# The issue order of all engines in a hybrid four-branch encoder block, computed with the framework's timeline model in place of its default model

## Chip, cores and metric

The kernel runs on one core of one Trainium2 chip. The metric is the time of one execution on the device, in microseconds. Five engines take part: TensorE (PE; its weight loads are shown as PEld), VectorE (DVE), ScalarE (ACT), GpSimd (POOL) and SyncE (SP), which here only issues DMAs. Each engine works off its own list of instructions strictly from the front; an instruction that needs a result of another engine waits for a semaphore, and everything behind it on that engine waits too.

## What is computed

One layer of a streaming encoder on 512 tokens of width 1024, float32 throughout. Cut to what matters:

```
h = rms_norm(x, norm_mix)
proj = h @ w_in                        # feeds four token mixers and four gates
y_ssd, y_lru, y_ret, y_rwkv = mamba2(...), rglru(...), retention(...), rwkv7(...)
merged = sum over m of sigmoid(gate_m) * (y_m @ w_branch[m])
x = x + merged @ w_out
h = rms_norm(x, norm_ffn)
x = x + (silu(conv(h @ up_gate)) * conv(h @ up_val)) @ w_down
return rms_norm(x, norm_final)
```

The part that matters here is rwkv7: per head, a state is carried from token to token. The kernel does this in 8 chunks of 64 tokens, one chunk after the other.

## The kernel before

**Products.** Every weight block is loaded by a DMA on SP's queue into `raw` (L106, four buffers), cast to fp32r by ACT into `whi` (L100) and its rest computed by DVE into `wlo` (L101); there are three buffers of each. A product is three matmuls (L119, L120, L121) for each of the 8 slices of the inner dimension, 128x128 weights against 512 columns, so 24 matmuls to a block, summed in a PSUM tile `acc` (three buffers). In the tail of the program (output projection, feed-forward) the same is done by lines 240 to 242 and 949 to 951. All other matmuls are plain fp32 and small; the profile counts two instructions for each of them.

**Rounds.** `rwkv` runs over 8 pairs of heads (j = 0 to 7, called rounds here). A round is:

- `rwkv_a1`: three projections (r, k, v), a norm (L313, then the square root on eight columns, L132 to L136), two small products (L125, L126).
- `rwkv_a2`: 16 fp32 matmuls (L372) whose results go through DRAM (writes L415, reads L418) into `nt`; then **the substitution**, 31 pairs of DVE instructions (L424, L426), each needing the one ahead of it, and a copy (L428); its result goes through DRAM again (L432, L433, L438, L441) into `x11` and `tt`.
- `rwkv_b`: 16 small matmuls (L452), a copy, 16 more (L462), a copy, and then **the chain** of 8 chunks. In a chunk PE does L480 (twice), DVE copies (L482), PE does L484, ACT and then DVE copy (L485, L486), PE does L488, DVE adds (L491), and that is the input of the next chunk's L480. Behind the chain stand 8 matmuls (L497), a norm on DVE (L506 to L514), a transpose (L96, into `rb`), a gate product and a write to DRAM (L246).

```
for c in range(NCH):
    nc.tensor.matmul(ps[...], g[:, c, e], sv[:, c, e, :], ...)      # L480
    nc.vector.tensor_copy(out=pp[:, c], in_=ps[...])                # L482
    nc.tensor.matmul(sk[:, 0:P], tt[:, c, :], pp[:, c], ...)        # L484
    nc.scalar.copy(out=sv[0:64, c, 0], in_=sk[0:64, 0:64])          # L485
    nc.vector.tensor_copy(out=sv[64:128, c, 1], in_=sk[64:128, ..]) # L486
    nc.tensor.matmul(sk[:, P:2 * P], bt[:, c, :], sv[:, c], ...)    # L488
    nc.vector.tensor_tensor(out=sv[h, c + 1, e], ..., op=ALU.add)   # L491
```

**Filler.** Between the rounds `fill(us)` pulls pieces of other work from a generator: the other three mixers, and then gates and branch products of those three (`branch`, which reads a mixer's output back from DRAM, L872, splits it into `yh` and `yl`, and multiplies it). Only the fourth branch product (`branch(3, 3, merged)`) needs the rounds' output; its inner slice 7 needs round 7. After it come the output projection, a norm, and the feed-forward products.

**What sets the order.** The code is traced into a program, and the framework then orders it. It plays the program on a model of the machine: whenever an engine of the model is free, it takes of the instructions whose inputs are there the one traced first, and the order in which that happens is the order in which each engine's instructions are issued on the chip. The times that `fill` is given and the order of the mixers only set the order of tracing. The model is chosen where the program's context is opened:

## Time and profile before

| | |
|---|---|
| median of 3 runs | 1616.52 us (1614.81 to 1617.13) |
| the profiled execution | 1615.14 us, of which the span from first to last instruction is 1613.4 us |
| PE busy in the span | 1562.6 us |
| DVE, ACT, POOL busy | 1047.2, 719.7, 141.2 us |
[...]

Busy means that at least one instruction of the engine was under way. Consecutive matmuls overlap, so the start of the next one tells what a matmul costs, and the duration doesn't. Waits are put down to what ended last.

### The profile page before, as it was taken

What the parts mean: (1) busy time and instruction counts of PE and PEld (TensorE: products, weight loads), DVE (VectorE), ACT (ScalarE), POOL (GpSimd) and SP (SyncE); (2) the same over time, 40 slices, a digit from 0 to 9 for tenths busy, and PEclk for the clock granted to TensorE, in tenths of its full rate; (3) what the DMA queues carried; (4) which work ended last, traced back from release to release, by engine and by line L of the source; (5) the groups of instructions that cost most, each with busy time, mean ns of one, the idle gap of its engine ahead of it and who ended that gap; (6) DMA issues with size and microseconds to landing.
All of it is one profiled execution on the core that took longest, in us unless ns stands there. A gap on an engine that the chain in (4) does not pass through costs nothing.

```text
span 1613.4 us, 22510 instructions
## 1 busy us (share of the span) xinstructions
PE 1562.6 (97%) x8452; PEld 1279.7 (79%) x8452; DVE 1047.2 (65%) x2302; ACT 719.7 (45%) x1188; POOL 141.2 (9%) x190
## 2 busy tenths in 40 slices
PE   7899999899999999999999999999999999999998
PEld 7787778787788788877788778788888888888886
DVE  6787697875886788878636757544435665656233
ACT  6453466445753576258422432323223544444122
POOL 1200202202101201201200300100000000000000
PEclk9999999999999999999999999999999999999999
DMA  5233133232243234433533323444222223233231
GB/s 205 92 122 99 56 118 91 76 107 87 87 125 97 77 105 116 125 105 101 163 105 105 118 91 99 133 140 142 91 92 92 94 92 104 91 102 106 95 102 53
DMA packets 108461, 169.47 MB, mean 105 GB/s; under 512 B 54832, under 2 KB 64304, under 8 KB 108352
## 3 DMA queue, kind: packets, MB, share of 16 engines
q1 hardware_dynamic: 107632, 166.92, 33.0%
q8 instruction: 66, 1.08, 0.3%
q10 hardware_dynamic: 720, 1.11, 0.2%
q14 instruction: 43, 0.35, 0.1%
HBM read 150.66 MB, written 15.24 MB: 103 GB/s over the span
## 4 chain that ended last, share of the span: by engine, by line
PE 79%; DVE 14%; ACT 3%; issue 2%; POOL 1%; DMA 1%; SPq 0%; DVEq 0%; ACTq 0%; POOLq 0%
PE acc L119 17%; PE acc L120 17%; PE acc L121 17%; PE acc L949 3%; PE acc L951 3%; PE acc L950 3%; DVE wlo L101 2%; PE rb L480 2%; PE acc L242 2%; PE acc L241 2%; PE acc L240 2%; PE ra L372 1%; PE rb L488 1%; PE inn L96 1%; PE ra L96 1%
## 5 line engine op out<-in xcount | busy, mean ns | idle before, releaser
L119 PE MATMUL acc<-hh,whi 128*128 128x512 f32 (+1 forms) x1240 | 487.3, 393 | 0.0
L120 PE MATMUL acc<-hh,wlo 128*128 128x512 f32 (+1 forms) x1240 | 486.0, 392 | 1.2 <-DVE wlo L101 1.1
L121 PE MATMUL acc<-hl,whi 128*128 128x512 f32 (+1 forms) x1240 | 485.9, 392 | 0.0
L101 DVE TENSOR_TENSOR wlo<-raw,whi 128x1024 fp32r<-128x1024 f32 x228 | 279.1, 1225 | 169.7 <-ACT whi L100 168.8
L100 ACT CAST whi<-raw 128x1024 fp32r<-128x1024 f32 x228 | 237.8, 1045 | 205.9 <-PE acc L951 86.5
L120 PEld LDWEIGHTS acc<-hh,wlo 128*128 128x128 f32 x1240 | 234.3, 189 | 45.6 <-issue 2.2
L119 PEld LDWEIGHTS acc<-hh,whi 128*128 128x128 f32 x1240 | 234.3, 189 | 44.6 <-issue 2.2
L121 PEld LDWEIGHTS acc<-hl,whi 128*128 128x128 f32 x1240 | 234.2, 189 | 44.3 <-issue 1.8
L1004 DVE SCALAR_TENSOR_TENSOR fc<-acc,fw,fc 128x511 f32<-128x511 f32 x88 | 65.9, 749 | 76.5 <-ACT fc L1002 75.0
L119 PE MATMUL acc<-yh,whi 128*128 128x512 f32 x256 | 102.4, 400 | 0.0
L120 PE MATMUL acc<-yh,wlo 128*128 128x512 f32 x256 | 101.1, 395 | 0.0
L121 PE MATMUL acc<-yl,whi 128*128 128x512 f32 x256 | 100.9, 395 | 0.0
L477 POOL TENSOR_SCALAR sd<-sv,dl 64x64 f32<-64x64 f32 x112 | 57.4, 513 | 351.4 <-DVE sv L491 338.0
L1002 ACT ACTIVATE fc<-acc,fw 128x512 f32<-128x512 f32 x44 | 34.3, 779 | 93.9 <-PE acc L121 93.9
L240 PE MATMUL acc<-whi,hh 128*128 128x256 f32 (+1 forms) x256 | 74.8, 293 | 0.4 <-ACT whi L100 0.4
L241 PE MATMUL acc<-wlo,hh 128*128 128x256 f32 (+1 forms) x256 | 74.4, 291 | 0.0
L242 PE MATMUL acc<-whi,hl 128*128 128x256 f32 (+1 forms) x256 | 74.1, 290 | 0.0
L949 PE MATMUL acc<-whi,gh 128*128 128x512 f32 x176 | 69.4, 395 | 0.0
L951 PE MATMUL acc<-whi,gl 128*128 128x512 f32 x176 | 69.4, 395 | 0.0
L950 PE MATMUL acc<-wlo,gh 128*128 128x512 f32 x176 | 69.4, 395 | 0.0
L878 ACT ACTIVATE gt<-acc 128x512 f32<-128x512 f32 x32 | 19.0, 597 | 91.0 <-PE acc L121 91.0
L424 DVE TENSOR_TENSOR prod<-nt,xr 128x60 f32<-128x60 f32 (+24 forms) x248 | 54.0, 218 | 5.5
(329 smaller groups left out, 2404.8 us busy)
## 6 DMA issues: line engine op xcount, KB each, us to landing
raw<-in_wts_dram SPq DMA_DIRECT2D x226, 512.0 KB, 3.3
yr<-y SPq DMA_DIRECT2D x32, 256.0 KB, 2.8
y<-sm SPq DMA_DIRECT2D x24, 256.0 KB, 2.2
nt<-nd SPq DMA_DIRECT2D x32, 128.0 KB, 3.2
sm<-acd SPq DMA_DIRECT2D x16, 256.0 KB, 3.6
x<-in_x_dram SPq DMA_DIRECT2D x4, 512.0 KB, 5.3
ym<-bg SPq DMA_DIRECT2D x16, 128.0 KB, 1.8
sm<-sm SPq DMA_DIRECT2D x32, 64.0 KB, 2.0
```

The source lines that it names most:

```text
L100: nc.scalar.copy(out=hi, in_=src)
L101: nc.vector.tensor_tensor(out=lo, in0=src, in1=hi.bitcast(F32), op=ALU.subtract)
L119: nc.tensor.matmul(ps, wh, xh, start=first, stop=False)
L120: nc.tensor.matmul(ps, wl, xh, start=False, stop=False)
L121: nc.tensor.matmul(ps, wh, xl, start=False, stop=last)
L240: nc.tensor.matmul(o, hh[:, ko, t], wh[:, s], start=ko == 0, stop=False)
L241: nc.tensor.matmul(o, hh[:, ko, t], wl[:, s], start=False, stop=False)
L242: nc.tensor.matmul(o, hl[:, ko, t], wh[:, s], start=False, stop=ko == KT - 1)
L949: nc.tensor.matmul(ps[i], xh[:, ko, t], w[0][:, s], start=ko == 0, stop=False)
L950: nc.tensor.matmul(ps[i], xh[:, ko, t], w[1][:, s], start=False, stop=False)
L951: nc.tensor.matmul(ps[i], xl[:, ko, t], w[0][:, s], start=False, stop=ko == 2 * nblk - 1)
L1004: nc.vector.scalar_tensor_tensor(out=t[:, s:], in0=ps[:, :S - s], scalar=fw[:, o + 2 - s:o + 3 - s], in1=t[:, s:], op0=ALU.mult, op1=ALU.add)
```

## The change

The context is opened with another model, the framework's timeline simulation, which follows sequencers, queues and engines more finely than the default one:

```diff
-    with _tile.TileContext(nc) as tc:
+    with _tile.TileContext(nc, schedule_with_timeline_sim=True) as tc:
         tile_hybrid_block(tc, *args)
```

The matmuls, vector operations, activations and DMAs are the same ones; ACT loads its function tables 65 times in place of 64, and instructions that only wait for a semaphore follow from the new order. The order differs on every engine, from the first norm to the last product. Three places are shown.

**Round 7, first chunk, on PE.** `g`, `sv`, `tt`, `bt`, `nt` belong to the chain, `acc` to the products. Before:

```order
L462 MATMUL rb<-tt,x_9774 32x32
L480 MATMUL rb<-sv,g 128x64 x2
L121 MATMUL acc<-hl,whi 128x512
L462 MATMUL rb<-tt,x_9774 32x32 x15
L119 MATMUL acc<-hh,whi 128x512
L120 MATMUL acc<-hh,wlo 128x512
L121 MATMUL acc<-hl,whi 128x512
L119 MATMUL acc<-hh,whi 128x512
L484 MATMUL rb<-nt,tt 128x128
```

And now:

```order
L121 MATMUL acc<-yl,whi 128x512 x2
L452 MATMUL rb<-x_9774,ab 32x32 x16
L462 MATMUL rb<-tt,x_9774 32x32 x16
L480 MATMUL rb<-sv,g 128x64 x2
L484 MATMUL rb<-nt,tt 128x128
L488 MATMUL rb<-sv,bt 128x128
L480 MATMUL rb<-sv,g 128x64 x2
```

The products that stood between the steps of this chain stand ahead of it; all 8 chunks of round 7 follow each other as the first one does.

**End of round 7, on PE.** `o` is the normed output of the round, `glh` the gate, `yh` the operand of the branch products. After the change:

```order
L480 MATMUL rb<-sv,g 128x64 x2
L484 MATMUL rb<-nt,tt 128x128
L497 MATMUL rb<-sv,gb 128x128 x8
L96 MATMUL rb<-ident,o 128x128 x4
L119 MATMUL rb<-glh,lh_10173 128x512
L120 MATMUL rb<-glh,ll_10174 128x512
L121 MATMUL rb<-gll,lh_10173 128x512
L119 MATMUL acc<-yh,whi 128x512
```

The `yh` of the last row is slice 7 of the fourth branch product, which is round 7's own output read back from DRAM; before the change gates and branch products of other mixers stood at each of these places.

**Substitution of round 5, on DVE.** `prod`, `nt`, `xr` belong to the substitution, `kss`, `knr`, `knu` to the norm of round 6's `rwkv_a1`. Before:

```order
L424 TENSOR_TENSOR prod<-nt,xr 128x18x4
L426 TENSOR_TENSOR xr<-xr,prod 128x18x4
L424 TENSOR_TENSOR prod<-nt,xr 128x17x4
L426 TENSOR_TENSOR xr<-xr,prod 128x17x4
L424 TENSOR_TENSOR prod<-nt,xr 128x16x4
L426 TENSOR_TENSOR xr<-xr,prod 128x16x4
```

And now:

```order
L101 TENSOR_TENSOR wlo<-raw,whi 128x1024
L315 TENSOR_SCALAR kss<-ra 128x8
L424 TENSOR_TENSOR prod<-nt,xr 128x17x4
L132 TENSOR_SCALAR knr<-kss 128x8
L426 TENSOR_TENSOR xr<-xr,prod 128x17x4
L134 SCALAR_TENSOR_TENSOR knu<-knr,kss 128x8
L424 TENSOR_TENSOR prod<-nt,xr 128x16x4
L135 TENSOR_TENSOR knu<-knu,knr 128x8
L426 TENSOR_TENSOR xr<-xr,prod 128x16x4
```

The norm of the next round and weight splits have moved in between the pairs of the substitution.

## Rows read from the trace of the kernel before

**Rows 1.** The page: busy time of each engine, and the chain that ended last.
```profile
PE 1562.6 (97%) x8452; PEld 1279.7 (79%) x8452; DVE 1047.2 (65%) x2302; ACT 719.7 (45%) x1188; POOL 141.2 (9%) x190
...
PE 79%; DVE 14%; ACT 3%; issue 2%; POOL 1%; DMA 1%; SPq 0%; DVEq 0%; ACTq 0%; POOLq 0%
```

**Rows 2.** Waits of PE: engine, line, waited for: total us, times, longest us.
```profile
PE inn L96 <- DVE nxn L157: 10.2, 1, 10.2
PE ra L372 <- DVE bk L357: 4.5, 1, 4.5
...
PE rb L488 <- DVE sv L486: 3.8, 4, 2.3
...
PE rb L497 <- DVE sv L486: 1.5, 1, 1.5
...
PE rb L480 <- DVE sv L491: 1.2, 3, 0.7
...
PE rb L484 <- DVE nt L482: 1.0, 3, 0.4
```

**Rows 3.** Timeline of PE, round 7: start us, duration us, engine, line, tiles, [wait].
```profile
962.55 1.05 PE L372 MATMUL ra<-g,bk 128*128 128x128 f32 x8
963.36 0.48 PE L121 MATMUL acc<-hl,whi 128*128 128x512 f32 x1
963.68 0.40 PE L119 MATMUL acc<-hh,whi 128*128 128x512 f32 x1
963.91 0.39 PE L120 MATMUL acc<-hh,wlo 128*128 128x512 f32 x1
...
1008.31 0.28 PE L452 MATMUL rb<-x,ab 32*32 32x32 f32 x2 [0.18 <-DMA x<-xd]
```

**Rows 4.** Timeline of DVE, round 7's substitution, first instruction and last.
```profile
977.27 0.21 DVE L424 TENSOR_TENSOR prod<-nt,xr 128x31 f32<-128x31 f32 x1
...
998.61 0.41 DVE L428 COPY prod<-xr 128x256 f32<-128x256 f32 x1
```

**Rows 5.** Groups of DVE from 970 to 999 us: count, busy us, mean ns, idle ahead.
```profile
L424 DVE TENSOR_TENSOR prod<-nt,xr 128x60 f32<-128x60 f32 (+24 forms) x31 | 6.7, 215 | 0.9
...
L101 DVE TENSOR_TENSOR wlo<-raw,whi 128x1024 fp32r<-128x1024 f32 x5 | 6.1, 1222 | 2.9 <-ACT whi L100 2.6 <-issue 0.3
```

**Rows 6.** Timeline of SP's queue, round 7: the four reads into nt.
```profile
966.41 1.71 SPq L418 DMA_DIRECT2D nt<-nd  x4
```

**Rows 7.** DMA issues: count, KB each, median us from issue to landing.
```profile
yr<-y SPq DMA_DIRECT2D x32, 256.0 KB, 2.8
...
nt<-nd SPq DMA_DIRECT2D x32, 128.0 KB, 3.2
...
y<-yu SPq DMA_DIRECT2D x8, 256.0 KB, 2.4
```

**Rows 8.** Timeline of PE, round 5: a chunk without products between its steps.
```profile
774.79 0.49 PE L484 MATMUL rb<-nt,tt 128*128 128x128 f32 x2
777.58 0.49 PE L488 MATMUL rb<-sv,bt 128*128 128x128 f32 x2 [2.30 <-DVE sv L486]
778.38 0.84 PE L480 MATMUL rb<-sv,g 128*128 128x64 f32 x4 [0.31 <-DVE sv L491]
779.60 0.80 PE L484 MATMUL rb<-nt,tt 128*128 128x128 f32 x2 [0.38 <-DVE nt L482]
```

**Rows 9.** Timeline of PE, round 5: the shortest step from L484 to L488.
```profile
785.69 0.38 PE L484 MATMUL rb<-nt,tt 128*128 128x128 f32 x2
...
786.69 0.49 PE L488 MATMUL rb<-sv,bt 128*128 128x128 f32 x2
```

**Rows 10.** Stretch 779 to 785.6 us: PE, PEld, DVE, ACT, POOL busy, clock, DMA.
```profile
779.00:785.60 6.60, 6.22 (x20) 5.16 (x20) 2.81 (x8) 0.74 (x3) 1.32 (x3) 0.50 0.41 138
```

**Rows 11.** Timeline of PE, end of round 7.
```profile
1045.69 1.09 PE L497 MATMUL rb<-sv,gb 128*128 128x128 f32 x8
...
1054.94 0.63 PE L96 MATMUL rb<-ident,o 128*128 128x128 f32 x4 [0.40 <-DVE o L514]
```

**Rows 12.** Timeline of SP's queue, end of round 7: the write of its output.
```profile
1057.93 0.33 SPq L246 DMA_DIRECT2D y<-yu  x1
```

## Prediction, written before the changed kernel ran

> **What bounds the kernel now.** I read the page first: PE is busy for 1562.6 of 1613.4 us and the chain that ended last runs through PE for 79% [rows 1], so the time is PE's work plus PE's waits. The list of PE's waits is short: its 23 groups add up to 44.3 us. Of these 10.2 are the first transpose waiting for the first norm, which no order avoids; the steps of the chain of chunks cost 3.8, 1.5, 1.2 and 1.0, together 7.5; the other 26.4 are waits ahead of L372, of transposes and of small matmuls, the largest 4.5 [rows 2]. L452, which needs the whole substitution and four DMA trips, waited once, for 0.18 us [rows 3]. So the old order hides the rounds almost wholly, and a new order can win little but lose much. I then read from the changed order how much PE work stands between the ends of each dependence, and from the trace how long the dependence takes. PE work is priced by starts: a product matmul of 512 columns is 0.23 us (963.68 to 963.91), four fp32 matmuls of 128 columns 0.81 to 0.89 (962.55 to 963.36, or to their end less the overlap) [rows 3].
>
> **Part 1: from L372 to L452.** This stretch is: the last L372 ends at 963.60 [rows 3]; four reads into nt are issued from 966.41 on, the last 1.3 later, and land 3.2 after their issue [rows 6, 7]: 7.3 us. Then the substitution. From its first instruction at 977.27 to the end of the copy at 999.02 [rows 4] it takes 21.75; its own instructions are 31 pairs of 0.215 each and the copy, 13.7 [rows 4, 5], and the others that stand between the first and the last of them in DVE's order, each at its own duration in the trace (a weight split 1.22 [rows 5]), are 6.9. So it takes what DVE has in that piece of its list, plus 1. From there to L452 at 1008.31 are another 9.3 [rows 3, 4]. The bill is therefore 17.6 + own + others. In the order before it is never more than the PE work that stands between L372 and L452: rounds 0 to 7 have 69, 50, 46, 59, 57, 53, 51 and 45 us of it against bills of 67, 48, 40, 55, 43, 46, 36 and 38, which agrees with the one wait of 0.18.
>
> In the changed order PE has 48.7, 63.5, 51.1, 43.1, 58.4, 39.6, 54.9 and 23.6 us there. Own work is unchanged, but others are now 26.6, 36.7, 29.4, 22.3, 29.6, 17.5, 21.0 and 4.8 us: the norm of the next round's a1, its scan and its splits stand between the pairs. The bills become 59.7, 67.9, 60.7, 53.4, 60.9, 48.7, 52.4 and 36.1. Bill less work: 11.0, 4.4, 9.6, 10.3, 2.5, 9.1, 0 and 12.5, together 59 us of new waits at L452. Bounds: 45, if each of the seven trips through DRAM that count here is 2 us shorter than in round 7; 80, if L424 also waits for what stands ahead of it, as in round 7 of before, where it began some 6 us after its data (966.41 + 1.3 + 3.2 = 970.9 against 977.27) [rows 4, 6, 7].
>
> **Part 2: chunks without cover.** Between the steps of the chain the old order has at least one product matmul, but for three steps. In the new one 24 steps to L480, 19 to L488 and 20 to L484 follow directly, 22 of these 63 in round 7, 41 in rounds 0 to 5. What such a step costs is seen at 774.79: 2.79 us to L488, less 0.22 of work; 0.80 to L480, less 0.22; 1.22 to L484, less 0.34 [rows 8]. That is the upper end, 2.57, 0.58 and 0.88. The shortest step to L488 in the trace took 1.00, less 0.22 [rows 9], and for the others I take the mere waits, 0.31 and 0.38 [rows 8], as lower end. Sums: 24 x 0.31 + 19 x 0.78 + 20 x 0.38 = 30, and 13.9 + 48.8 + 17.6 = 80. In round 7 no other instruction stands between the chain's own on DVE, so I go nearer to the lower end: 0.5, 1.2 and 0.6, together 47. Less the 7.5 that the chain waits now [rows 2]: 39 (22 to 73).
>
> The rest of the chains is the reverse: in round 6 a whole product block, some 5 us, stands between any two steps. That costs nothing by itself but delays the round: its chain takes 118 us of PE work where it took 30. That is why round 7 comes last and alone: the fillers are used up, and the fourth branch product needs round 7's output.
>
> **Part 3: the end of round 7.** Behind L497 comes the norm: from L497's end at 1046.78 to the transpose at 1054.94 are 8.2 us [rows 11], of which 1.2 is a split of other work; say 7. Then 3.0 to the write at 1057.93 [rows 11, 12], 2.4 until it lands, 2.8 for reading it back [rows 7], 1.3 for the two splits, less 1.6 of own PE work: 7.9. With some 1 us for each of the copies ahead of L462, L484 and L497: 18 us (14 to 20), all in the open, since the products that covered it now stand ahead of it.
>
> **Part 4: what is won.** The 26.4 us of other waits [rows 2]: the new order has more PE work ahead of many of these (round 0: 15 to 20 us from L125 to L372, where 9 stood), so I take off 20 (0 to 26). Fewer switches: PE goes from small fp32 matmuls to products 219 times, before 396. After such a switch the next product starts 0.32 instead of 0.23 later [rows 3], though the last small matmul gives part of it back; 177 times 0 to 0.09 is 0 to 16, I take 7.
>
> **Part 5: the clock.** Right after the uncovered chunk the granted clock was 0.50, the lower of the two levels, for 6.6 us [rows 10], in which PE works at half pace: 3.3 us lost. Over the whole span the mean clock was 0.993 of full speed, which is 11 us in all. New waits bring new stretches, but most of round 7 is waiting, and that doesn't get slower: +5 (0 to 20).
>
> **The sum.** 1615.1 for the profiled execution + 59 + 39 + 18 - 20 - 7 + 5 = 1709; the median of before is 1.4 above that execution, so **1710 us**, 5.8% slower. All lower ends together give 1654, all upper ones 1808; they won't all fall one way.
>
> **Rivals.** *The new order wins*: the waits of part 4 go with their clock stretches, and the substitution runs at the pace that the new order assumes. For this the bills must be no more than the work ahead of them, so that own + others take 37 instead of 45 us in the mean of the first three rounds, against DVE durations read from the trace. It speaks for it that the list of waits holds 26 us which a better order could hide; against it that round 7 alone has 12.5 + 18 us and 22 uncovered steps, which at the lower prices (7 x 0.31 + 7 x 0.78 + 8 x 0.38) are 11 more. With nothing lost but round 7's part 3 and these 11 it gives 1615 - 26 - 7 - 10 + 18 + 11 = 1601. It turns at parts 1 to 3 being worth less than 43 us together, where their lower ends sum to 81. 4%.
>
> *No difference*: losses of some 43 us cancel against what is won; needs nearly the same. 3%.
>
> *Only round 7 hurts*: if other instructions in the DVE list wait less than they take now, and the DMA trips overlap the substitution, the waits of rounds 0 to 5 shrink to a third: 1615 + 12.5 + 15 + 25 + 18 - 20 - 7 = 1658. 18%.
>
> *The clock takes more*: each of the seven waits at L452, the end of round 7 and about a dozen groups of uncovered steps is followed by a stretch like that at 779, 20 x 3.3 = 66 in place of 5: 1771. For it: the one uncovered chunk that the trace has was followed by it at once [rows 10]. Against it: the list holds dozens of waits, and the 11 us that the mean clock stands for are the price of three or four such stretches. 15%. [...]
>
> **How the numbers follow.** 60% for the forecast, 1665 to 1760; 18% for the rival with round 7 alone, 1635 to 1665; 15% for the clock, 1750 to 1800; 4% and 3% for faster and the same. The range 1648 to 1782 leaves out these 7, a third of the third rival and about 6 of 100 at the top. A measurement of this kernel tells 0.2% from no change: faster 4%, same 3%, slower 93%.
>
> **What would show it.** PE's waits should be led by L452, L484, L488, L480 and by the L119 behind round 7; six or seven waits at L452 of 3 to 13 us; a stretch of some 100 us from round 7's L372 on in which PE has only about a third of its work; the tail behind it, from the output projection on, as long as before. L372's 4.5 us should be gone. The sum is wrong if L452 finds its data ready, which would mean that DVE gets through its list without the waits I count, or if the products are short of weights, a wait that hardly exists now and that I give nothing for.

## The result, and the profile of the changed kernel

The changed kernel takes 1825.18 us (median of 4 runs, 1821.71 to 1828.49) where the kernel before takes 1616.29 in the same comparison: a ratio of 1.129, 95% interval 1.127 to 1.132. It is slower, as forecast, but by 209 us in place of 94, and 43 us above the upper end of the range.

The page of its profiled execution: busy time of each engine, PE's busy tenths and the granted clock in 40 slices, and the chain that ended last.

```profile
span 1826.7 us, 22530 instructions
...
PE 1642.2 (90%) x8452; PEld 1355.0 (74%) x8452; DVE 1058.4 (58%) x2302; ACT 724.6 (40%) x1189; POOL 143.4 (8%) x190
...
PE   7988879888989878987899899996589999999998
...
PEclk9998889889989888978899899998589999999999
...
PE 75%; DVE 10%; ACT 7%; DMA 4%; issue 3%; SPq 1%; POOL 0%; DVEq 0%; ACTq 0%; POOLq 0%
```

Held against [rows 1], PE is busy 79.6 us longer with the same 8452 instructions, and it stands still for 1826.7 - 1642.2 = 184.5 us where it was 50.8. The first is the clock: its mean is 0.918 of full speed, before 0.993, and the digits below 9 are spread over the first three quarters of the program. Summed over its stretches, the clock stands at 0.50 for 298 us, before for 22. PE is busy in 206 of these; at half pace, half of that is lost: 103 us, before 9 ([rows 10] showed one such stretch). I call this the **lost pace**, and span less PE's busy time the **waits**; what is left is PE's work at full clock. Half is a round figure: in the changed kernel products start 0.43 us apart at 0.50 (458.67 to 459.10) against 0.23 at 1.00 (448.34 to 448.57), so an estimate from these starts is 0.465 of the busy time, or 96 us in place of 103.

PE's waits in the changed kernel: engine, line, waited for: total us, times, longest us.

```profile
PE rb L452 <- DMA x<-xd: 23.6, 6, 15.7
PE rb L488 <- DVE sv L486: 20.4, 21, 4.5
PE acc L119 <- ACT sm L604: 18.7, 5, 8.0
PE rb L484 <- DVE nt L482: 15.5, 21, 3.4
PE inn L96 <- DVE nxn L157: 10.1, 1, 10.1
PE acc L119 <- ACT yh L100: 9.1, 3, 6.5
PE rb L96 <- DVE o L514: 8.0, 1, 8.0
PE rb L480 <- DVE sv L491: 7.5, 24, 0.4
PE acc L119 <- ACT sm L681: 7.0, 5, 2.3
```

Against [rows 2] the first norm's 10 us stand as they did and L372's 4.5 are gone. L452 and the chain's steps lead, as forecast. Not forecast is `acc`: L119, the first matmul of a product, waits for L604 and L681, which are ACT's evacuations of gate products of two mixers (RG-LRU and retention). Before, L119 had no wait worth a row; now all its waits are 38.6 us, 25.7 of them for these two. And behind the rows shown stands a long tail of small ones: 139 waits over 0.3 us, before 30.

Round 7, PE's timeline: start, duration, engine, line, tiles, wait. It answers to [rows 3] and [rows 11].

```profile
1279.34 0.28 PE L452 MATMUL rb<-x,ab 32*32 32x32 f32 x2 [15.72 <-DMA x<-xd]
...
1286.68 0.79 PE L488 MATMUL rb<-sv,bt 128*128 128x128 f32 x2 [0.68 <-DVE sv L486]
1287.78 1.11 PE L480 MATMUL rb<-sv,g 128*128 128x64 f32 x4 [0.31 <-DVE sv L491]
1289.27 0.80 PE L484 MATMUL rb<-nt,tt 128*128 128x128 f32 x2 [0.38 <-DVE nt L482]
...
1314.73 3.15 PE L497 MATMUL rb<-sv,gb 128*128 128x128 f32 x16
1325.85 1.09 PE L96 MATMUL rb<-ident,o 128*128 128x128 f32 x4 [7.97 <-DVE o L514]
...
1334.71 0.80 PE L119 MATMUL acc<-yh,whi 128*128 128x512 f32 x1 [6.49 <-ACT yh L100]
```

This part is as drawn in the prediction: the wait at L452, bare steps at 0.31, 0.38 and 0.68, then the norm and the trip of `y` through DRAM. What wasn't drawn is the duration column: L488 takes 0.79 and L480 1.11, where at full clock L488 takes 0.49 [rows 8] and the first L480 of run bare7, below, 0.66.

The same stretch and four others as windows: us, then busy time and count of PE, PEld, DVE, ACT and POOL, granted clock, DMA share, GB/s. The first is the time at 0.50 around round 7; then L452 to the last L497 of rounds 0, 3 and 6; then L372 to L452 of round 7.

```profile
1266.04:1317.24 51.20, 25.85 (x138) 19.81 (x139) 12.61 (x56) 3.10 (x12) 5.30 (x12) 0.50 0.06 8
...
162.69:255.45 92.76, 76.50 (x402) 60.08 (x402) 46.45 (x105) 41.10 (x74) 12.62 (x16) 0.85 0.21 71
...
614.34:714.80 100.46, 79.89 (x409) 63.75 (x409) 53.25 (x99) 52.26 (x87) 11.35 (x16) 0.85 0.24 76
...
1092.87:1234.27 141.40, 141.40 (x723) 117.96 (x723) 64.78 (x100) 41.26 (x62) 9.99 (x16) 1.00 0.33 109
1241.77:1279.34 37.57, 21.86 (x105) 17.82 (x104) 24.71 (x89) 6.36 (x11) 1.90 (x1) 0.82 0.31 82
```

In rounds 0 and 3 PE lacks 16 and 21 us in that window, and the clock is 0.85. In round 6, where the filler is gates and branch products and no mixer is left, nothing is lost, though there too 21 to 31 matmuls stand in one piece between any two steps of the chain.

All such windows, summed by stretch, against the terms of the prediction (us; waits and lost pace before and after):

| stretch | waits | lost pace | extra, forecast | extra, measured |
|---|---|---|---|---|
| L372 to L452, rounds 0 to 6 | 11.6, 42.2 | 1.7, 17.7 | 46.5 (part 1) | 46.6 |
| the same, round 7 | 1.1, 15.7 | 0, 0 | 12.5 (part 1) | 14.6 |
| L452 to L497, rounds 0 to 6 | 8.5, 71.8 | 4.9, 63.4 | 22.3 (part 2) | **121.8** |
| the same, round 7 | 0, 12.0 | 0, 12.9 | 16.7 (part 2) | 24.9 |
| from there to the end | 7.8, 26.7 | 0, 7.4 | 18 (part 3) | 26.3 |
| the rest | 21.6, 16.0 | 2.4, 1.7 | -20 (part 4) | -6.3 |
| work at full clock | | | -7 (part 4) | -14.6 |
| clock, anywhere | | | 5 (part 5) | in the rows above, 94.2 |
| sum | 50.7, 184.5 | 9.0, 103.2 | 94 | 213.3 |

So 100 us of the miss lie in one row. Of its 121.8, 58.5 are lost pace, 28.5 are new waits of the chain's own steps and of L497 (7.5 before, 36.0 now), and some 35 are new waits of other work in the same stretches: 16.1 of L119, 6.6 of transposes (L96), 4.1 of L663 and smaller ones. The row of work at full clock is a remainder and carries the error of taking half for the lost pace; with 0.465 it would be -8.

### The profile page after: what moved, and what is told of

It is laid out like the page before. It is cut to its first block, busy times and chain, and to the rows that moved or that the text cites. A ratio compares the mean times of both kernels' runs of the same rounds, so it can differ in the third digit from the quotient of the medians.

```text
span 1826.7 us, 22530 instructions
## 1 busy us (share of the span) xinstructions
PE 1642.2 (90%) x8452; PEld 1355.0 (74%) x8452; DVE 1058.4 (58%) x2302; ACT 724.6 (40%) x1189; POOL 143.4 (8%) x190
## 3 DMA queue, kind: packets, MB, share of 16 engines
q10 hardware_dynamic: 720, 1.11, 0.2%
## 4 chain that ended last, share of the span: by engine, by line
PE 75%; DVE 10%; ACT 7%; DMA 4%; issue 3%; SPq 1%; POOL 0%; DVEq 0%; ACTq 0%; POOLq 0%
PE acc L119 17%; PE acc L120 17%; PE acc L121 16%; PE acc L949 3%; PE acc L951 3%; PE acc L950 3%; PE rb L480 1%; PE acc L240 1%; DVE wlo L101 1%; PE acc L242 1%; PE acc L241 1%; PE ra L372 1%; PE rb L484 1%; PE rb L488 1%; DVE bk L357 1%
## 5 line engine op out<-in xcount | busy, mean ns | idle before, releaser
L119 PE MATMUL acc<-hh,whi 128*128 128x512 f32 (+1 forms) x1240 | 493.7, 399 | 29.0 <-ACT sm L604 18.7
L121 PE MATMUL acc<-hl,whi 128*128 128x512 f32 (+1 forms) x1240 | 488.0, 396 | 0.0
L119 PEld LDWEIGHTS acc<-hh,whi 128*128 128x128 f32 x1240 | 241.5, 195 | 81.5 <-ACT sm L604 20.3
L120 PEld LDWEIGHTS acc<-hh,wlo 128*128 128x128 f32 x1240 | 241.2, 195 | 46.5 <-issue 0.7
L121 PEld LDWEIGHTS acc<-hl,whi 128*128 128x128 f32 x1240 | 238.8, 194 | 48.4 <-issue 1.1
L1004 DVE SCALAR_TENSOR_TENSOR fc<-acc,fw,fc 128x511 f32<-128x511 f32 (+1 forms) x88 | 65.8, 749 | 78.3 <-ACT fc L1002 76.8
L119 PE MATMUL acc<-yh,whi 128*128 128x512 f32 x256 | 101.7, 398 | 9.6 <-ACT yh L100 9.1
L121 PE MATMUL acc<-yl,whi 128*128 128x512 f32 x256 | 100.5, 397 | 0.0
L424 DVE TENSOR_TENSOR prod<-nt,xr 128x60 f32<-128x60 f32 (+24 forms) x248 | 55.4, 223 | 15.7 <-DMA nt<-nd 11.3
L119 PEld LDWEIGHTS acc<-yh,whi 128*128 128x128 f32 x256 | 48.4, 189 | 21.1 <-ACT yh L100 10.7
```

The costliest lines, as they stand in the source:

```text
L119: nc.tensor.matmul(ps, wh, xh, start=first, stop=False)
L120: nc.tensor.matmul(ps, wl, xh, start=False, stop=False)
L121: nc.tensor.matmul(ps, wh, xl, start=False, stop=last)
L1004: nc.vector.scalar_tensor_tensor(out=t[:, s:], in0=ps[:, :S - s], scalar=fw[:, o + 2 - s:o + 3 - s], in1=t[:, s:], op0=ALU.mult, op1=ALU.add)
```

## Experiments

The edits are shortened to what they do. Most of them hold an engine's list fixed. The kernel is traced once with one model, its lists are read off, and in a second trace the chosen engines are tied to them while the chosen model orders the rest:

```
for names in pinned:                       # one list for each pinned engine
    for a, b in zip(names, names[1:]):
        tc.add_manual_dep(traced[b], a, NoSync, reason="pinned")   # issue order only
...
nc = build(True, [order(build(False), "PE")])    # new model, PE's list as before
```

All results, with the profiled execution's waits, mean clock and lost pace:

| run | what differs | us | waits | clock | lost pace |
|---|---|---|---|---|---|
| before | | 1616.3 | 50.7 | 0.993 | 9.0 |
| changed | | 1825.2 | 184.5 | 0.918 | 103.2 |
| bare7 | old order, round 7's chain bare | 1646.2 | 67.9 | 0.978 | 23.3 |
| warm_old | old order, 553 idle matmuls | 1677.0 | 49.6 | 0.995 | 5.8 |
| warm_new | new order, the same | 1818.1 | 141.3 | 0.960 | 60.5 |
| warm_new2 | the same, better placed | 1805.4 | 129.3 | 0.958 | 58.0 |
| x_pe | new model, old list of PE | 1752.7 | 146.4 | 0.969 | 47.0 |
| x_dve | new model, old list of DVE | 1939.1 | 244.5 | 0.907 | 137.0 |
| x_act | new model, old list of ACT | 1932.2 | 238.9 | 0.910 | 130.8 |
| x_pe_act | new model, old lists of PE, ACT | 1708.4 | 117.0 | 0.976 | 35.4 |
| x_pe_dve | new model, old lists of PE, DVE | 1675.3 | 86.6 | 0.979 | 32.2 |
| y_pe | old model, new list of PE | 1870.7 | 220.5 | 0.912 | 107.8 |
| hold7 | new model, last filler kept for round 7 | 1810.3 | 172.5 | 0.927 | 96.4 |
| fine_new | new model, chains of rounds 0 to 6 evenly filled | 1834.3 | 209.5 | 0.924 | 81.2 |
| fine_old | old model, the same list of PE | 1849.5 | 220.3 | 0.917 | 92.5 |
| tables | new order, 39 table loads fewer | 1798.1 | 165.9 | 0.927 | 93.6 |
| gate_own | new order, L604 into a tile of its own | 1812.2 | 174.3 | 0.926 | 94.5 |

### Is the clock a cause or a by-stander?

**bare7** makes one small piece of the change in the old order.

```diff
+    at = [k for k, n in enumerate(old) if n in own]          # own: all of round 7's rwkv_b
+    piece = old[at[0]:at[-1] + 1]
+    piece = [n for n in piece if n not in own] + [n for n in piece if n in own]
+    nc = build(False, [old[:at[0]] + piece + old[at[-1] + 1:]])
```

> The default model with PE's list pinned to that of the kernel before, but for one piece: the products that stood between round 7's first L452 and its last L497 stand ahead of that L452, so the chain of round 7 is bare, as in the new order; rounds 0 to 6 and the end of round 7 are as before. By the prediction's part 2 without the clock: 8 x 0.5 + 7 x 1.2 + 8 x 0.6 = 17 us, 10 to 31, so 1626 to 1648. If the clock falls for the length of the chain, 10 to 16 us more: 1640 to 1660, and the profile shows the chain at 0.50.

The edit goes further than this text: `own` is all of `rwkv_b`, with the transposes and the gate product behind the chain, so the products that stood between L497 and the transposes are moved ahead too, and the end of round 7 is not as before.

Measured: 1646.2, ratio 1.017 (1.014 to 1.020). Its PE timeline around the start of the chain and at the wait behind it, and the window of the chain:

```profile
1040.69 0.39 PE L121 MATMUL acc<-yl,whi 128*128 128x512 f32 x1
1041.00 1.10 PE L452 MATMUL rb<-x,ab 32*32 32x32 f32 x32
1042.57 0.24 PE L462 MATMUL rb<-tt,x 32*32 32x32 f32 x2 [0.47 <-ACT x L456]
...
1045.06 0.80 PE L484 MATMUL rb<-nt,tt 128*128 128x128 f32 x2 [0.82 <-ACT tt L465]
1046.54 0.80 PE L488 MATMUL rb<-sv,bt 128*128 128x128 f32 x2 [0.68 <-DVE sv L486]
1047.64 1.12 PE L480 MATMUL rb<-sv,g 128*128 128x64 f32 x4 [0.31 <-DVE sv L491]
...
1084.85 1.09 PE L96 MATMUL rb<-ident,o 128*128 128x128 f32 x4 [7.02 <-DVE o L514]
```

```profile
1047.00:1077.00 30.00, 21.07 (x70) 15.93 (x70) 7.57 (x30) 1.44 (x7) 5.28 (x12) 0.50 0.00 1
```

The chain's waits are 11.0 us, at the lower end of part 2. But the clock went to 0.50 at 1044.47, in the wait ahead of the first L484, when PE had just done the small matmuls L452 to L480. It stayed there to the end of the chain at 1077.83, with no wait longer than 0.82 us, and on through a wait of 7.02 us for the norm until 1088.84, 44 us in all. From L452 to L497 that is 11.0 us of waits and 11.6 us of lost pace. Over the run, 17.2 us of new waits (11.0 in the chain, most of the rest the transpose behind L514) came with 14.3 us of lost pace. The time alone would not decide: 1646.2 lies in both ranges, and some 9 us of it come from the bared end, without which it would be about 1638. What decides is the profile, with the chain at 0.50 and its lost pace between the 10 and 16 us named.

**warm_new** and **warm_old** put idle matmuls ahead of the instructions that wait.

```diff
+def warm(nc, hh, ps, *at):                  # at: line, round, chunk
+    for _ in range(WARM.get(at, 0)):
+        nc.tensor.matmul(ps[:, 256:512], hh[:, 0, 0:P], hh[:, 0, 0:256], start=True, stop=True)
...
-            sk = rb.tile([P, S], F32, name="rb")
+            sk = rb.tile([P, S], F32, name="rb"); warm(nc, hh, sk, 484, j, c)
```

> The new order, all five lists pinned to it, with 553 idle matmuls (constant operands, 256 columns, 0.12 us each at full clock, results used by nobody) put on PE ahead of those instructions of the rounds that waited in the trace of the new kernel: as many at each place as fill 90% of its wait (125 ahead of round 7's L452, 60 ahead of its last transposes, 2 to 34 at steps of the chains). That adds 66 us of work inside some 78 us of waits. Theory 1 (much of the loss is the clock, which falls where PE stands still in the rounds): the low clock falls from 298 us to 100 to 200, PE's own work gets shorter by 35 to 60 us, the time is 1765 to 1790 although work was added. Theory 2 (the clock is a by-stander: what PE gains it waits out at the next result): 1815 to 1840, however much the low clock shrinks. No change of the low clock at all would say that it hangs on something else than these waits.

> The order of the kernel before, all five lists pinned to it, with the same 553 idle matmuls at the same places of the rounds, where PE hardly waits. The control for their price: all of them are work in the open, 553 x 0.12 = 66 us and for each of the some 70 groups a switch of 0 to 0.09: 1680 to 1690 by both theories.

The control cost 61 us, a little under its 1680 to 1690. In the new order the low clock fell from 298 to 146 us, as theory 1 has it, but the time, 1818.1, lies in the range of theory 2, and its ratio of 1.125 (1.120 to 1.129) is not clear of the change's 1.129 (1.127 to 1.132). So this run leaves it open. One reason is visible in the waits: the idle matmuls ahead of L488 waited for L486 themselves (21.4 us), because L486 still read their PSUM tile. **warm_new2** writes these into `ps`, the chunk's other tile.

> As the run with 553 idle matmuls in the new order, but those ahead of L488 write into the other PSUM tile of the chunk, which nobody reads any more; in the run before, they waited for the copy L486 themselves and stood in the open. Theory 1 (the clock's share turns into time): 17 us more of waits are filled and some 15 us more of the low clock go, 1785 to 1805, against 1825 without any idle matmul. Theory 2 (the clock is a by-stander): 1815 to 1835.

Measured: 1805.4, ratio 1.116 (1.112 to 1.119), clear of the change's, 0.4 us above the range of theory 1 and 10 below that of theory 2. What is left of the waits at L452 and L488 (23.6 and 20.4 in the changed kernel):

```profile
PE rb L452 <- DMA x<-xd: 2.9, 2, 2.4
...
PE rb L488 <- DVE sv L486: 2.4, 5, 0.8
```

The books balance: work at full clock rises by 75.9 us (the idle matmuls; in warm_old it was 63.9, and the 12 us between them weren't looked into), waits fall by 55.2, lost pace by 45.2, the span by 24.5. The lost pace did turn into time; had the clock been a by-stander, it would have come back as waits. No run pins the new order and changes nothing else, but in two later runs that pin it (tables and gate_own) the waits that they don't aim at stand as they did: L488's are 20.5 and 19.7 us against 20.4.

### Which engine's list?

**x_pe**, **x_dve**, **x_act** undo one list each, **y_pe** makes PE's alone.

> The new model with PE's list pinned to the order of the kernel before; DVE, ACT, POOL and SP are ordered by the new model around it. Theory 1 (the loss sits in PE's list: whole product blocks between the steps of the chain, rounds that come later and later, no filler left for round 7): the cover is back, so PE's waits fall from 184 us to near the 51 of before, the low clock from 298 us to under 40, and the time is 1616 to 1650. Theory 2 (the loss sits in the lists of DVE and ACT, which mix the next round's a1 and the mixers into the substitution and the chain): the results still come late, PE now waits for them at fixed places, 1700 to 1800.

> The new model with DVE's list pinned to the order of the kernel before; the others are ordered by the new model around it. Theory 1 (PE's list): PE is still free to put product blocks between chain steps, 1750 to 1830. Theory 2 (DVE's list): the substitution runs at its old pace and the chain's copies come at once, waits at L452, L484 and L488 go (some 70 of 134 us) with the low clock that follows them, 1640 to 1720.

> The new model with ACT's list pinned to the order of the kernel before; the others are ordered by the new model around it. Theory 1 (PE's list) and theory 2 in its form with DVE's list alone: 1750 to 1830. If ACT's list is at fault (table loads of the mixers' functions ahead of the copies that free acc, 18.7 and 7.0 us of waits of L119 for L604 and L681): these waits go with some 20 us of low clock, 1720 to 1770.

> The reverse: the default model as before, with PE's list pinned to the new order; the other engines are ordered by the default model around it. Theory 1 (PE's list): slow as the new kernel, 1770 to 1830, with round 7 alone and uncovered. Theory 2 (lists of DVE and ACT): round 7 alone stays (some 60 us), the waits of rounds 0 to 6 go, 1660 to 1700.

DVE's or ACT's list can't be undone alone: with its old list in the new order the time is 1939 and 1932, worse than the change itself. In x_dve products wait for weight splits, which that list brings at other places:

```profile
PE acc L120 <- DVE wlo L101: 35.4, 20, 5.8
```

PE's new list alone, with everything else ordered around it by the old model, costs more than the change (1871): to lose the time, this list is enough. Its old list wins back 72 us of 209. This one time, 1753, lies in the range of theory 2, whose late results it shows; the other three lie above every range that was named, so neither theory holds as it stands. The longest waits of x_pe are for results of DVE:

```profile
PE rb L488 <- DVE sv L486: 16.5, 15, 3.6
PE rb L484 <- DVE nt L482: 13.8, 12, 2.2
PE rb L480 <- DVE sv L491: 12.1, 7, 4.2
```

> The new model with the lists of PE and DVE pinned to the order of before, ACT, POOL and SP ordered by the new model around them. PE's list alone gave 1753, with waits of the chain's steps for DVE (L488 16.5, L484 17.0, L480 12.4 us). Theory (lists must fit each other; the rest of that run's loss is DVE's list): these waits go with their clock, 1620 to 1670. Rival (ACT's list holds the rest): 1700 to 1760.

> The new model with the lists of PE and ACT pinned to the order of before, DVE, POOL and SP ordered by the new model around them. Theory (the rest of the loss of the run with PE's list alone is DVE's list): 1690 to 1760, the chain's waits for DVE stay. Rival (ACT's list): 1620 to 1670.

1675 and 1708: DVE's list on top of PE's wins 77 us, ACT's 44. The one came out some 5 us above its range, the other inside. The orders on the engines are one plan; DVE's and ACT's old lists, which cost over 100 us alone, win once PE's stands beside them.

### What in PE's list costs it?

**hold7** asks whether round 7's want of filler is the main thing.

```diff
+        mark = [i for i in nc.cur_bb.bb.instructions if str(i.engine).endswith('.PE')][-1]   # end of rwkv_a2(j)
...
-    fill(1e6)
+    with tc.issue_after(mark): fill(1e6)
```

> The new model, but the last piece of filler (what is traced behind round 7: part of the second branch product and the third) may not be issued on PE ahead of round 7's L372 products. Theory (round 7 alone, with 42.6 us of waits and 15.6 us of low clock in the new kernel, is a quarter of the loss, the rest lies in rounds 0 to 6): 1765 to 1785. If the want of filler in round 7 were the main thing: under 1700. If what is held back is missed in round 6 instead: 1800 to 1830.

1810.3, the last of the three cases: the waits and lost pace of round 7, from L372 to L497, fell from 40.6 to 19.0 us, and 10 us of that came up again in round 6. Round 7 is not the main part: in the table above its three rows make 66 us of the 213.

**fine_new** and **fine_old** ask whether it is the uneven placing of the products in rounds 0 to 6. Count of other matmuls between the steps of round 3's chain (L480, L484, L488 in turn), in the order before, in the new one, and evenly spread:

```
before    7  6  3  8  3  2  3  3  2  3  4  2  3  3  2  3  3  3  3  8  3  5
new      21 21 14  1  1  0  0  0  0 19 22 22 23 25 21 16  4  8  0  0  0  2
even     10  9 10  9 10  9 10 10  9 10  9 10  9 10  9 10 10  9 10  9 10  9
```

> The new model with PE's list pinned to the new one, but in the chains of rounds 0 to 6 the same other instructions stand spread evenly between the chain's steps (7 to 23 in each gap, where now 0 to 38 stand); round 7 and all else as in the new list. Theory E (the uneven placing is the cause): the chain's waits in rounds 0 to 6 (36 us) go and with them half of the 63 us of low clock there, 1750 to 1775. Theory M (the mixers' late results and the lists of ACT and DVE are the cause): the chain's waits go, but those of L119 and of the mixers' matmuls stay or grow, and the clock falls with them, 1795 to 1840.

> The same list of PE, spread evenly, with the other engines ordered by the default model around it; to be held against 1871 for the uneven list with that model. Theory E: 1780 to 1810. Theory M: 1840 to 1890.

1834.3 and 1849.5, both in theory M's ranges: theory E falls. The even list wins 21 us with the old model around it and nothing with the new one. Waits of fine_new:

```profile
PE acc L119 <- ACT sm L604: 31.6, 5, 11.5
...
PE acc L119 <- ACT sm L681: 21.8, 6, 4.5
...
PE rb L488 <- DVE sv L486: 5.8, 9, 0.7
```

In L452 to L497 of rounds 0 to 6 the chain's waits went from 36 to 3 us as wanted, and L119's rose from 16 to 45. What the chain no longer waits for, the products wait for.

### Why do the buffers come late?

L119 needs one of three PSUM buffers. Two of them hold the RG-LRU's gate products until L604 evacuates them, and L604 writes over `xc`, which is ready only when L586's result has gone through ACT (L587 to L600) and DVE (L601). For the four pairs, time from the last L586 to the first L604, and how many L119 start in it:

| | us | L119 started |
|---|---|---|
| before | 11.2, 11.6, 10.1, 10.4 | 16, 11, 9, 15 |
| changed | 10.6, 10.6, 11.3, 11.8 | 0, 2, 0, 0 |

The latency is the same; the cover is gone. ACT in the changed kernel ahead of the wait of 8.03 us that ended at 457.23:

```profile
449.80 1.28 ACT L600 ACT_TABLE_LOAD   x1
451.10 0.63 ACT L600 ACTIVATE sm<-sm 128x512 f32<-128x512 f32 x1
451.63 1.03 ACT L100 CAST whi<-raw 128x1024 fp32r<-128x1024 f32 x1
452.68 1.28 ACT L334 ACT_TABLE_LOAD   x1
453.97 0.69 ACT L334 ACTIVATE cs<-ra,hwa 128x512 f32<-128x512 f32 x1
454.56 0.71 ACT L593 ACTIVATE sm<-sm,m 128x512 f32<-128x512 f32 x1
455.29 1.28 ACT L604 ACT_TABLE_LOAD   x1
456.58 0.60 ACT L604 ACTIVATE sm<-acc 128x512 f32<-128x512 f32 x1
```

Two suspects are in it: table loads, and the tile that L604 must wait for. **tables** takes away the first.

```diff
-            nc.scalar.activation(out=xc, in_=proj("lru_g", j), func=AF.Gelu_apprx_tanh)
+            nc.scalar.activation(out=xc, in_=proj("lru_g", j), func=AF.Tanh)
```

(and Silu to Tanh, Sqrt to Square in the mixers)

> All five lists pinned to the new order; the mixers' Gelu, Silu and Sqrt are replaced by Tanh, Tanh and Square (so the mixers' outputs are others), which takes 39 of ACT's 65 table loads away, 1.28 us each, 50 us of ACT. Theory A (the new waits of products for a PSUM buffer, L119 for L604 and L681, 25.7 us, come from table loads ahead of the instructions that free it): these waits fall to under 10 us, other mixers' waits by some 10, and the clock with them: 1775 to 1800. Theory B (they come from ACT's and DVE's waits for each other, with the substitution in between, not from the loads): 1810 to 1825.

1798.1, ratio 1.112 (1.108 to 1.116), inside theory A's range at its upper edge. The wait for L604 fell, but only to 8.5, and with 2.5 for L681 the two are 11.0, a little over the 10 of theory A:

```profile
PE acc L119 <- ACT sm L604: 8.5, 4, 5.2
```

**gate_own** takes away the second and leaves the loads.

```diff
-            nc.scalar.activation(out=xc, in_=proj("lru_g", j), func=AF.Gelu_apprx_tanh)
-            nc.vector.tensor_tensor(out=a2, in0=a2, in1=xc, op=ALU.mult)
+            gg = fl.tile([P, S], F32, name="lg", bufs=2)
+            nc.scalar.activation(out=gg, in_=proj("lru_g", j), func=AF.Gelu_apprx_tanh)
+            nc.vector.tensor_tensor(out=a2, in0=a2, in1=gg, op=ALU.mult)
```

> The lists of PE, DVE, POOL and SP pinned to the new order; L604 writes into a tile of its own in place of the one that L601 reads, and ACT's list is ordered by the new model around that, so the Gelu can follow its product at once and give the PSUM buffer back. Theory (the new list has put the gate products ahead of the L586 whose results, over ACT and DVE, the Gelu needs, and the 10 us until then are without cover on PE because two of three buffers are held): L119's waits for L604 fall from 18.7 to under 4 us, and the clock gives some 0.7 us for each: 1790 to 1810. Rival (the buffers are late because ACT itself is late, with table loads and casts ahead): 1815 to 1830.

1812.2, ratio 1.121 (1.117 to 1.125), just above the range. No wait for L604 is left; one of 4.7 us at L119 came in its place:

```profile
PE acc L119 <- DVE prod L424: 4.7, 1, 4.7
```

The first Gelu of each of the four pairs now starts 10 to 17 us ahead of the end of the last L586 instead of 10 to 12 behind it. So the tile was what held the buffers (18.7 us of waits for L604 with it shared, none with a tile of its own); the loads made it longer (8.5 us with 39 fewer of them). L119's waits fell by 14.4 us of 38.6, the time by 13. The other waits of the mixers in the row of 121.8 (L96, L663, L656, L792, L586) are small and many and weren't taken apart; that they come about in the same way isn't shown.

## Why the prediction was wrong

**Part 5, the clock, is the step that failed first.** It gave 5 us (0 to 20); measured are 94.2, so 89 of the 119 us by which the forecast missed; waits that parts 1 to 4 had too small make 38, and the remainder of work at full clock takes 8 off. The argument was that new waits bring few new low stretches, because the dozens of waits in the old list cost only 11 us in all, and that in round 7 waiting doesn't get slower. bare7 shows both to be wrong: one bare chain with its bare end brought 44 us at 0.50 and 14.3 us of lost pace, for 17.2 us of waits. Over the whole of bare7 that is 0.83 us of lost pace for a us of new wait; in the changed kernel it is 0.70, in x_pe_dve 0.65, in x_pe and x_pe_act 0.40. The waits of the old list were no measure: of its 30 over 0.3 us, 23 have no other within 5 us, of the 139 in the changed kernel 18. That they cost little because they stand alone isn't tested by a run. With bare7's ratio on the 116 us of parts 1 to 3, part 5 would have been 96 and the forecast 1801. The rival with the clock (1771, 15%) was the nearest case: it had 66 us in 20 stretches, and there are 28 stretches of 3.4 to 51.2 us with 103 us of lost pace. In bare7's chain the clock fell and stayed low among waits of at most 0.82 us.

**Part 4 is the second.** It took 20 us of other waits off, on the ground that more PE work stands ahead of many of them. Those waits did go in part (L372 from 8.3 to 1.0), but by lines, 133.7 us of new waits less 23.4 at L452, 38.7 in the chain and 14.1 at the end of round 7 leave some 57 us more for all the others, where -20 was forecast. (The rows of the list that it started from add up to 43.2, not 44.3, so the other waits were 25.5, not 26.4.) I had set bill against cover for the rounds alone. The mixers have such bills too, L586 to L604 for one, and the new order had moved their cover away just as it had moved the chain's. The remark at the end, that products short of weights would spoil the sum, looked in the right direction, but for 25.7 of L119's 38.6 us it was PSUM buffers that they were short of.

**Part 1 held in its size, less so in its form.** The eight stretches from L372 to L452 took 60.9, 66.6, 62.9, 50.6, 61.9, 49.7, 53.1 and 37.6 us against bills of 59.7, 67.9, 60.7, 53.4, 60.9, 48.7, 52.4 and 36.1, and cost 61.2 us more than before against 59. But L452 itself waited for 23.6 us, 16.8 of them in round 7. In rounds 0 to 6 PE lost most of that time ahead of it, at products and mixers and to the clock (16.0 of the 61.2 are lost pace); whether L452 would have waited as billed without these losses isn't shown, so the agreement of 61 with 59 may be luck in part. The upper bound of 80 wasn't worked out: 6 us more in each of seven rounds would be 101.

**Part 2, the price of a bare step, was good:** L480, L484 and L488 rose by 40 us against 39. That the sum fits so well is luck in part: round 7's stretch waited 12.0 us (16.7 forecast; bare7's 11.0), rounds 0 to 6 28.5 more at these steps (22.3 forecast). What the term lacked was the clock on top of it. That whole blocks between two steps cost nothing by themselves is right as well: in round 6 PE was busy for 141.40 of 141.40 us, at 1.00.

**Part 3**, 18 us, was 8.0 at the transpose and 6.5 at the product that needs round 7's output, with 7.4 of lost pace and some smaller waits: 26.3. **The fewer switches**: work at full clock fell by 14.6 in place of 7, or by 8 with the finer price of the lost pace. That the switches made it isn't shown: x_act and x_dve, with 204 and 231 changes from small matmuls to products by their traces, have 1561 and 1559 us of such work, the changed kernel, with 223, has 1539, and the kernel before, with 404, has 1554.

**The rivals.** That the new order wins, or that nothing changes, was rightly put low. That only round 7 hurts is refuted by the table: 168 us of the extra time lie in rounds 0 to 6.

## What to carry to other kernels

Price a new wait of TensorE together with the clock: in the slower orders here each us of new wait brought another 0.40 to 0.83 us of lost pace, and inside a bare chain about one (11.6 for 11.0 in bare7). So look at the granted clock of the nearest bare stretch before you call it small. When a scheduler moves cover, write the bill against the cover for every chain that crosses engines and holds a buffer, the filler's too, not only for the chain that looks critical. And treat the lists of the engines as one plan: undoing a single one can be worse than the change itself (1939 and 1932 against 1825).

## What the runs showed of the hardware that I had not expected

In bare7 the clock fell without any long wait. It went from 1.00 to 0.50 at 1044.47, when the products had just given way to the small matmuls L452, L462 and L480, with one wait of 0.47 us among them and one of 0.82 under way, and stayed at 0.50 for the rest of the chain, while PE was busy for 21 of 30 us in the window shown. It rose again at 1088.84, 2.9 us after the end of the transposes (1085.94), behind which the products of L119 to L121 stand in PE's list.

And work for nobody paid here: 553 idle matmuls, which cost 61 us where nothing waits (warm_old), made the changed kernel 20 us faster (warm_new2), because they stood in waits and the time at the low clock fell from 298 to 153 us.
